# Gate columns summed on VectorE instead of multiplied on TensorE, and mixer steps given out by an account of VectorE's pending work

## The chip, the cores and the metric

The kernel runs on one core of a Trainium2 chip. The metric is device time in microseconds (us) of one execution. A core has engines that each work through their own queue of instructions in order: TensorE (PE in the profile, its weight loads PEld), VectorE (DVE), ScalarE (ACT), GpSimd (POOL) and SyncE (SP, which here only issues DMAs). They wait for each other by semaphores.

## The reference

One step of a diffusion backbone with one layer, 128 context tokens and 256 latent tokens, so T = 384 columns of tokens, with D = 4096 features.

```python
mod = (silu(c) @ w_ada + b_ada)            # for two conditions: c_ctx and c
shift, scale, gate = split(mod, 3)         # 4096 columns each
u = rms_norm(h, norm_w) * (1 + scale) + shift
proj = u @ w_in                            # 4096 x 16448
#   8 retention heads (q, k, v, g: 256 wide) and 16 gated DeltaNet heads (q, k, v, z: 128 wide)
#   DeltaNet: 5-tap conv on q, k, v; l2norm; chunked delta rule with a triangular solve;
#   both scans run forward and backward, from a cached state for the latent tokens
out = concat([o_ret, o_gdn]) @ w_out       # 4096 x 4096
h = h + gate * out
y = rms_norm(h, final_norm_w)
```

The outputs are y for both groups of tokens and the four new states of the context tokens. Only the third part of `mod`, the gate (4096 columns for two conditions), is touched by the arithmetic of the change. It is used at the very end, where the output projection is scaled by it.

## The kernel before

All large products are made in float32 with a split: each piece of weights (256 rows of one `raw` tile serve two pieces) is rounded on ScalarE (`wh`, `split_tile`, L210), the rest `wl = raw - wh` is made on VectorE (L211), and TensorE adds three products (L259 to L261 or L265 to L267) per tile of results. A piece is one step of 128 of the 4096 rows for 512 columns of weights. Four `raw` tiles, and five `wh` and five `wl` tiles, are in a ring, so weights are prepared some four pieces ahead of TensorE.

`run_pieces` walks through one long list of pieces, calls `prepare` of the pieces ahead and `compute` of the one in turn, and so sets the order of all queues when the program is built. The list has three stages:

1. Shift and scale of `mod` (class `Ada`, L323), and the first parts of the input projection as far as `u` is ready.
2. The remaining input projection: 32 groups of 512 columns, four for each p = 0 to 7. The first two give k, q and then v, z of the DeltaNet heads 2p and 2p+1 (kind "T", results 128x384), the other two q, k and v, gate of the retention head p (kind "N", results 128x512). When a group with k and q is done, the mixer that needs it (`gdn(p)` or `ret(p)`) is put on `bg_list`.
3. The output projection, eight groups of 512 columns. The mixers' outputs go through DRAM (`d_mix`) and come back in `mix_load`.

A mixer is a Python generator. Each `yield` ends a step: a few instructions on VectorE, ScalarE, TensorE (tiles named `bg`), GpSimd or a DMA. `gdn` has 127 steps: convolutions of k and q on VectorE (L645), norms, exponentials and masks, a triangular solve of 30 rounds on VectorE (L854 and L856, its input and output go through DRAM as `d_m` and `d_x`), merges of 32x32 blocks on TensorE, convolution of v, and the chunk products. `ret` has 34. A step leans on the one before it nearly everywhere.

Steps come into the queues in two ways. After every triple of products `slot(ns)` moves a planned clock on by 480 or 639 ns, and when the pause after the last step is over it calls `bg_step`, which takes one step of `urgent` or of the first mixer on `bg_list`. `pace` sets the pause from the step's declared cost, `PACE`, and the time left to the mixer's due time. The other way is `bg_drain(tag)`: it takes steps with nothing between them until that mixer is finished. It is called where something must be free or finished: in `new_raw` (eight result tiles, the oldest mixer's are wanted back), in `mix_load`, in `open_out`, and before a group of the output projection. Where the mixer is done already it does nothing.

Gate columns are made in stage 2 by eight `Ada` objects of 512 columns, 16 pieces each, mixed among the pieces of the groups of kind "N". A piece loads 512 KB of `w_ada` into a `raw` tile and issues four small products on four column strips of TensorE (tile `adg`, L323). At the end the four strips are copied (`gsb`, L1177), added by another product with `sel` (L1183), the bias is added (L1190) and the sums go to `d_gate` in DRAM.

Of the kernel before, what the change touches and what calls it, by code (L numbers as in the profile page):

```python
# [7 lines left out]
F32 = mybir.dt.float32  # L8
F32R = mybir.dt.float32r
AF = mybir.ActivationFunctionType  # L10
ALU = mybir.AluOpType
# [4 lines left out]
D = 4096  # L16
NK = 32
T = 384
# [26 lines left out]
PRE = 5  # L45
RING = 5
RAW_RING = 4
PACE = 1.4
CG = 166e3
CR = 45e3  # L50
COST = {"gates": 35e3, "gdn": CG, "ret": CR}
# [12 lines left out]

# [2 lines left out]
def hybrid_step(ctx: ExitStack, tc: tile.TileContext, x_prompt, x_sample, state_ret_fwd, state_ret_bwd,  # L67
# [33 lines left out]

    ident = const.tile([128, 128], F32, name="ident")
    half_c = const.tile([128, 2, 12], F32, name="half_c")
    mid_ctx = ExitStack()
# [5 lines left out]
    cst = mid.tile([128, 2 * NK + 32], F32, name="cst")  # L110
    sel = mid.tile([128, 2], F32, name="sel")
# [8 lines left out]
    rq_dec = mid.tile([128, 2, 2, 8], F32, name="rq_dec")  # L120
    rk_dec = mid.tile([128, 2, 8], F32, name="rk_dec")

    G.memset(half_c[:, 0], -0.5)
    G.memset(half_c[:, 1], 0.5)

# [20 lines left out]

    urgent = []

    clock = {"next": 0.0, "now": 0.0}
    left, due = {}, {}  # L150

    def pace(tag, ns):
# [13 lines left out]
    def bg_step():  # L166


        while urgent:
            try:  # L170
                return pace(("urgent", 0), next(urgent[0]))
# [14 lines left out]
    def slot(ns):  # L186
        clock["now"] += ns
        clock["next"] -= ns
        if clock["next"] <= 0:
            clock["next"] = max(clock["next"], -SLOT) + bg_step()  # L190


    def load_piece(src, chunks, k0, nk, ring=None):
        shape = [128, nk, len(chunks), chunks[0][1]]
# [6 lines left out]
                         in_=src[k0 * 128:(k0 + nk) * 128, c0:c0 + cn].rearrange("(k p) n -> p k n", p=128))  # L201
        return raw

    def split_tile(raw, shape, place=None):
# [5 lines left out]
        A.copy(h, raw)  # L210
        V.tensor_tensor(lo, raw, h.bitcast(F32), op=ALU.subtract)  # L211
        return h, lo

    class Gemm:
# [87 lines left out]
    class Ada:  # L302
# [3 lines left out]

        slots = 450.0

        def __init__(self, c0, width, ps_alloc, done, ring=None):
# [7 lines left out]
        def compute(self, i, raw):  # L317
            if self.ps is None:
                self.ps = self.ps_alloc()
            cs = slice(256 * (i // NK), 256 * (i // NK) + 256)  # L320
            for q in range(4):
                k = i % NK + q
                PE.matmul(self.ps[32 * q:32 * q + 32, cs], cst[:, 2 * k:2 * k + 32], raw[:, q, 0],  # L323
                          start=(k < 4), stop=(k >= NK - 4), tile_position=(0, 32 * q))
            slot(450)
            if i + 4 == self.width // 256 * NK:
                self.done(self.ps)
            return 1

    class Do:  # L330

# [16 lines left out]
    def run_pieces(pieces):  # L348

        t = 0.0  # L350
        for obj, i in pieces:
            if (id(obj), i) in dues:
                due[dues[id(obj), i]] = t
            t += obj.slots
        ready, nxt = {}, 0
        out = {"do": 0, "ada": 0, "w": 0}
        room = {"do": len(pieces), "ada": ADA_RING - 1, "w": RING - 1}
        kind = lambda o: "do" if isinstance(o, Do) else ("ada" if isinstance(o, Ada) and o.ring else "w")
# [21 lines left out]
    V.tensor_copy(sel, con[:, C_SEL:C_SEL + 2])  # L380

    def psb():
        return ps_st.tile([128, 512], F32, tag="s", name="s")
# [156 lines left out]
    def sum_done(g, partial, last):  # L540
# [9 lines left out]
        def done(n, ps):  # L550
            box = kept[g]
            if kind == "T":
                t = box[n // 2][:, T * (n % 2):T * (n % 2) + T]
                if partial:
                    V.tensor_tensor(t, ps, t, op=ALU.add)  # L555
                else:
                    A.copy(t, ps)
            else:
                for i in range(2):
                    t = box[i][:, 256 * n:256 * n + 256]  # L560
                    if partial:
                        V.tensor_tensor(t, ps[:, 256 * i:256 * i + 256], t, op=ALU.add)
                    else:
                        (A.copy if i else V.tensor_copy)(t, ps[:, 256 * i:256 * i + 256])  # L564
# [605 lines left out]
        yield  # L1170


    def gate_done(i):
        def done(ps):
            sb = [mx.tile([128, T], F32, tag="gsb", name="gsb", bufs=2)[:, 0:256] for _ in range(2)]
            for j in range(2):
                A.copy(sb[j], ps[:, 256 * j:256 * j + 256])  # L1177
            urgent.append(fin(ps, sb))

        def fin(ps, sb):  # L1180
            yield GATE
            for j in range(2):
                PE.matmul(ps[0:2, 256 * j:256 * j + 256], sel, sb[j], start=True, stop=True)  # L1183
            yield
            c0 = 512 * i
            for j in range(2):
                G.dma_start(out=sb[j][0:2], in_=b_ada[0, 2 * D + c0 + 256 * j:2 * D + c0 + 256 * j + 256].partition_broadcast(2))
            yield 2000
            for j in range(2):
                V.tensor_tensor(sb[j][0:2], ps[0:2, 256 * j:256 * j + 256], sb[j][0:2], op=ALU.add)  # L1190
                G.dma_start(out=d_gate[:, c0 + 256 * j:c0 + 256 * j + 256], in_=sb[j][0:2])
        return done
# [20 lines left out]
    ada_q = []  # L1213
    for i in range(8):
        ada_q += Ada(2 * D + 512 * i, 512, lambda: ps_main.tile([128, 512], F32, tag="mm3", name="adg"), gate_done(i)).pieces
    for g, (kind, chunks) in enumerate(groups):
        k0 = reached.get(g, 0)
        pre, done = sum_done(g, ("dram" if g >= 4 else "sbuf") if k0 else None, True)
        gm = Gemm(kind, w_in, chunks, list(range(k0, NK)), done, pre)
        if g % 4 == 0 and g:  # L1220
            dues[id(gm), max(0, len(gm.pieces) - PRE)] = ("gdn", g // 4 - 1)
        if kind == "T":
            pieces += gm.pieces
        else:
            n, rest = len(gm.pieces), 0
            if g % 2:
                rest = min(8, n // 2)
                cnt = len(ada_q) - 16 * (7 - g // 4)
            else:
                cnt = min(16, max(0, 16 * n // (n + NK - reached.get(g + 1, 0) - 8)))  # L1230
            pieces += gm.pieces[:LEAD] + interleave(gm.pieces[LEAD:n - rest], ada_q[:cnt]) + gm.pieces[n - rest:]
            ada_q = ada_q[cnt:]
    assert not ada_q
    rowk = [(2 * (j // 4) if j % 4 >= 2 else 16 + 2 * (j // 4)) + j % 2 for j in range(NK)]

    mixl = {}
# [14 lines left out]
    oc = {}  # L1251

    def open_out():
        bg_drain()
# [25 lines left out]
    def out_done(c0):  # L1280
# [3 lines left out]
        def pre():  # L1284
            if not oc:
                open_out()
            bg_drain(("out", c0 - 512))
            op = oc["sb"]
            box["x"] = op.tile([128, 3, 512], F32, tag="xo", name="xo", bufs=1)
            box["g"] = op.tile([128, 2, 512], F32, tag="go", name="go")  # L1290
            box["w"] = op.tile([128, 512], F32, tag="wo", name="wo")
# [22 lines left out]
    def place(i):  # L1314
# [2 lines left out]
        return m >= 0 and [t[m].rearrange("p k t -> p (k t)")[:, 0:512].rearrange("p (a b) -> p a b", a=2)  # L1317
                           for t in (uh, ul)]

    for i in range(8):  # L1320
        pre, done = out_done(512 * i)
        gm = Gemm("N", w_out, [(512 * i, 256), (512 * i + 256, 256)], list(range(NK)), done, pre,
# [5 lines left out]
        if i == 0:  # L1328
# [4 lines left out]
            for j, piece in enumerate(seq):  # L1333
                for m, fn in ((j - 2, mix_put), (j, mix_load)):
                    if 0 <= m < NK:
                        pieces += Do(lambda m=m, fn=fn: fn(m)).pieces
                pieces.append(piece)
        else:
            pieces += gm.pieces
    run_pieces(pieces)  # L1340
    bg_drain()

# [50 lines left out]
```

## Time and profile before

| | |
|---|---|
| median of 3 runs | 3338.46 us (3335.72 to 3339.66) |
| profiled execution, its own time | 3342.99 us |
| its span, first to last instruction | 3340.9 us |
| TensorE busy | 97% of the span |
| VectorE busy | 55% |
| ScalarE busy | 36% |
| GpSimd busy | 9% |
| granted clock of TensorE, mean | 0.994 |

Busy time is the time in which an engine has at least one instruction under way. A row of a group gives count, busy time and mean duration, and behind the second bar the engine's idle time just before those instructions with what ended most of it. Durations on one engine can overlap a little, so count times mean can exceed the busy time.

### The profile page before, as it was taken

How to read it: one execution, taken by the hardware profiler on the slowest of the kernel's cores; microseconds unless marked ns; L12 is line 12 of the kernel's file. 1: busy time of each engine (PE TensorE's matmuls, PEld its weight loads, DVE VectorE, ACT ScalarE, POOL GpSimd, SP SyncE). 2: the span in 40 equal slices, each digit the busy share in tenths (PEclk: the TensorE clock that was granted, in tenths of full speed). 3: DMA queues.
4: the chain of work that ended last, by engine and by line, in shares of the span. 5: the costliest groups of instructions: out<-in, count | busy, mean ns of one | idle time of the engine just before them, and what ended most of it. 6: DMA issues, size and time to landing. Idle time of an engine off the chain costs nothing. (4 is left out here: it accounts for less than half of the span.)

```text
span 3340.9 us, 51824 instructions
## 1 busy us (share of the span) xinstructions
PE 3256.4 (97%) x19312; PEld 2706.2 (81%) x19312; DVE 1840.7 (55%) x3811; ACT 1198.9 (36%) x2588; POOL 292.2 (9%) x463
## 2 busy tenths in 40 slices
PE   5999999999999999999999999999999999999998
PEld 2778888877699779789789779779779877788887
DVE  2554433335855756754856746746844845444444
ACT  3322222224245235244345245235244334333333
POOL 0000000001101001001011001011000012100000
PEclk9999999999999999999999999999999999999999
DMA  9888998975534554544645645554644556645444
GB/s 304 290 287 272 330 311 266 297 251 159 179 105 135 169 153 149 179 145 140 192 146 152 185 129 156 173 154 147 177 153 141 160 153 188 187 145 170 145 151 170
DMA packets 594236, 626.14 MB, mean 187 GB/s; under 512 B 38978, under 2 KB 577042, under 8 KB 593984
## 3 DMA queue, kind: packets, MB, share of 16 engines
q1 hardware_dynamic: 570096, 551.04, 52.7%
q0 software_dynamic: 23888, 71.79, 7.3%
q8 instruction: 151, 2.47, 0.3%
q14 instruction: 101, 0.83, 0.1%
HBM read 590.37 MB, written 32.33 MB: 186 GB/s over the span
## 5 line engine op out<-in xcount | busy, mean ns | idle before, releaser
L211 DVE TENSOR_TENSOR wl<-raw,wh 128x512 fp32r<-128x512 f32 x1274 | 854.3, 687 | 939.8 <-ACT wh L210 935.8
L210 ACT CAST wh<-raw 128x512 fp32r<-128x512 f32 x1274 | 756.6, 620 | 1350.6 <-DMA raw<-in_w_in_dram 659.0
L265 PE MATMUL mm<-wh,uh 128*128 128x512 f32 x1920 | 784.3, 408 | 9.1 <-ACT rawt L564 5.6
L266 PE MATMUL mm<-wl,uh 128*128 128x512 f32 x1920 | 755.3, 393 | 6.4 <-DVE wl L211 5.8
L267 PE MATMUL mm<-wh,ul 128*128 128x512 f32 x1920 | 752.9, 392 | 0.0
L259 PE MATMUL mm<-uh,wh 128*128 128x384 f32 x2048 | 721.0, 352 | 6.2 <-DVE ul L555 3.8
L261 PE MATMUL mm<-uh,wl 128*128 128x384 f32 x2048 | 689.4, 337 | 0.0
L260 PE MATMUL mm<-ul,wh 128*128 128x384 f32 x2048 | 688.8, 336 | 0.0
L265 PEld LDWEIGHTS mm<-wh,uh 128*128 128x128 f32 x1920 | 362.2, 189 | 141.0 <-issue 48.2
L259 PEld LDWEIGHTS mm<-uh,wh 128*128 128x128 f32 x2048 | 387.3, 189 | 51.2 <-issue 34.6
L266 PEld LDWEIGHTS mm<-wl,uh 128*128 128x128 f32 x1920 | 362.7, 189 | 81.2 <-DVE wl L211 14.1
L267 PEld LDWEIGHTS mm<-wh,ul 128*128 128x128 f32 x1920 | 362.2, 189 | 78.2 <-DVE ul L1248 0.7
L260 PEld LDWEIGHTS mm<-ul,wh 128*128 128x128 f32 x2048 | 387.6, 189 | 3.9 <-issue 2.9
L261 PEld LDWEIGHTS mm<-uh,wl 128*128 128x128 f32 x2048 | 386.8, 189 | 0.0
L854 DVE TENSOR_TENSOR tmp<-M 48x4 f32<-48x4 f32 (+14 forms) x240 | 189.3, 789 | 3.4
L323 PE MATMUL ada<-adar,cst 128*32 128x256 f32 x2048 | 147.5, 404 | 26.9 <-DMA adar<-in_w_ada_dram 26.9
L645 DVE SCALAR_TENSOR_TENSOR acc<-rawt,cw,acc 128x126 f32<-128x126 f32 (+3 forms) x384 | 133.8, 413 | 12.8 <-ACT acc L640 12.8
L266 PE MATMUL o<-wl,uh 128*128 128x512 f32 x354 | 138.1, 390 | 0.2 <-DVE wl L211 0.2
L265 PE MATMUL o<-wh,uh 128*128 128x512 f32 x354 | 138.0, 390 | 0.2 <-ACT wh L210 0.2
L267 PE MATMUL o<-wh,ul 128*128 128x512 f32 x354 | 137.9, 390 | 0.0
L323 PEld LDWEIGHTS ada<-adar,cst 128*32 128x32 f32 x2048 | 53.8, 112 | 92.7 <-DMA adar<-in_w_ada_dram 42.8
L856 DVE TENSOR_REDUCE M<-tmp 48x2 f32<-48x4 f32 (+14 forms) x240 | 121.6, 507 | 8.3
(321 smaller groups left out, 2522.7 us busy)
## 6 DMA issues: line engine op xcount, KB each, us to landing
raw<-in_w_in_dram SPq DMA_DIRECT2D x1028, 256.0 KB, 3.6
adar<-in_w_ada_dram SPq DMA_DIRECT2D x256, 512.0 KB, 5.7
raw<-in_w_ada_dram SPq DMA_DIRECT2D x128, 512.0 KB, 4.3
raw<-in_w_out_dram SPq DMA_DIRECT2D x256, 256.0 KB, 3.1
rawt<-d_part POOLq DMA_DIRECT2D x26, 384.0 KB, 4.3
d_part<-spill POOLq DMA_DIRECT2D x9, 768.0 KB, 7.4
gr<-d_gc POOLq DMA_DIRECT2D x16, 384.0 KB, 7.4
d_mix<-rawt POOLq DMA_DIRECT2D x32, 192.0 KB, 2.8
```

The source lines that it names most:

```text
L210: A.copy(h, raw)
L211: V.tensor_tensor(lo, raw, h.bitcast(F32), op=ALU.subtract)
L259: PE.matmul(ps, wh, high(k), start=st, stop=False)
L260: PE.matmul(ps, wh, low(k), start=False, stop=False)
L261: PE.matmul(ps, wl, high(k), start=False, stop=sp)
L265: PE.matmul(ps, a, h, start=st, stop=False)
L266: PE.matmul(ps, a, lo, start=False, stop=False)
L267: PE.matmul(ps, b, h, start=False, stop=sp)
L323: PE.matmul(self.ps[32 * q:32 * q + 32, cs], cst[:, 2 * k:2 * k + 32], raw[:, q, 0], start=(k < 4), stop=(k >= NK - 4), tile_position=(0, ...
L645: V.scalar_tensor_tensor(out=dst[:, lo:hi], in0=x[:, lo + o:hi + o], scalar=w(t), in1=dst[:, lo:hi], op0=ALU.mult, op1=ALU.add)
L854: V.tensor_tensor(t, M[0:48, 0:i, 0:i].rearrange("p j c -> p c j"), M[0:48, i:i + 1, 0:i].to_broadcast([48, i, i]), op=ALU.mult)
L856: V.tensor_reduce(M[0:48, i, 0:i], t, axis=AX.X, op=ALU.add)
```

## The change

The gate columns leave TensorE. A new class `GateSum` loads two row blocks of 384 columns of `w_ada` (384 KB, 16 loads per object) and adds each block, times the condition's value of that row, to a running sum on VectorE: two conditions, so four instructions of 128x384 per load, and for 4096 columns eleven objects with 704 instructions in all (64 of them 256 columns wide). At an object's end four small products with a tile of ones add over the partitions, and the bias and the store to `d_gate` follow. Half of a load's sums are put off behind the next split (`later`). Seven objects are mixed among the four groups of p = 1 to 7, four among groups 1 to 6 of the output projection.

The steps of mixers are given out by another rule. `clock["dve"]` is an account of when VectorE will be done with what was issued: each split, each sum and each step adds a declared cost. `slot` now takes a step only where that account is less than `BACKLOG` = 1500 ns ahead of the planned clock. `bg_drain` has no such condition, and its steps are put on the account too. The pause is also set otherwise: `PACE` 1.4 to 1.0, `FMAX` 1.0 to 2.0, and smaller declared totals.

```diff
-PACE = 1.4
-CG = 166e3
-CR = 45e3
+PACE = 1.0
+CG = 130e3
+CR = 28e3
+SPLIT = 690.0
+STEP = 300.0
+BACKLOG = 1500.0
-FMAX = 1.0
+FMAX = 2.0
+GATE_W = 384
+GATE_END = 10
...
+    def dve(ns):
+        clock["dve"] = max(clock["dve"], clock["now"]) + ns
...
         while bg_list:
             tag, job = bg_list[0]
             try:
-                return pace(tag, next(job))
+                ns = next(job)
+                dve(STEP if ns is None or ns < 0 else ns)
+                return pace(tag, ns)
...
     def slot(ns):
         clock["now"] += ns
         clock["next"] -= ns
-        if clock["next"] <= 0:
+        if clock["next"] <= 0 and clock["dve"] - clock["now"] < BACKLOG:
             clock["next"] = max(clock["next"], -SLOT) + bg_step()
...
         V.tensor_tensor(lo, raw, h.bitcast(F32), op=ALU.subtract)
+        dve(SPLIT)
+        if later:
+            later.pop(0)()
...
+    class GateSum:
+        def prepare(self, i):
+            raw = load_piece(w_ada, [(2 * D + self.c0, self.width)], i, 2)
...
+            def add(q):
+                for v, acc in enumerate(self.acc):
+                    dve(1.5 * self.width)
+                    a, w = acc[:, 0:self.width], cst[:, 2 * (i + q) + v:2 * (i + q) + v + 1]
+                    if i + q == 0:
+                        V.tensor_scalar(a, raw[:, q, 0], scalar1=w, scalar2=None, op0=ALU.mult)
+                    else:
+                        V.scalar_tensor_tensor(out=a, in0=raw[:, q, 0], scalar=w, in1=a, op0=ALU.mult, op1=ALU.add)
...
+        def fin(self):
...
+            ps = ps_main.tile([128, T // 2], F32, tag="mm3", name="gsum")
+            for r, v, o in parts:
+                PE.matmul(ps[r:r + 32, 0:n], ones, self.acc[v][:, o:o + n], start=True, stop=True, tile_position=(0, r))
...
-    def gate_done(i):
...
+    gate_sums = [GateSum(c0, min(GATE_W, D - c0)).pieces for c0 in range(0, D, GATE_W)]
...
+        if p:
+            gp = gp[:LEAD] + interleave(gp[LEAD:-GATE_END], gate_sums.pop(0)) + gp[-GATE_END:]
...
+            pieces += interleave(behind, [p for ps in gate_sums for p in ps]) + gm.pieces
```

The order of the queues changes at many places. The first shown is TensorE's queue in `gdn(5)`, between the merges of blocks. Before, the mixer's products (`bg`) stand one step at a time between products of the projection (`mm`); L916 and L926 are two merges.

```order
L265 MATMUL mm_20195<-wh,uh_1784 128x512
L266 MATMUL mm_20195<-wl,uh_1784 128x512
L267 MATMUL mm_20195<-wh,ul_1785 128x512
L926 MATMUL bg<-U,P_20388 64x64 x12
L265 MATMUL mm_20196<-wh,uh_1784 128x512
L266 MATMUL mm_20196<-wl,uh_1784 128x512
L267 MATMUL mm_20196<-wh,ul_1785 128x512
```

In the changed kernel the same merge (now L1005) stands among the mixer's other products, from the first transposes (L858) to the last; there is no `mm` row in this stretch of 164 products.

```order
L972 MATMUL bg<-P_20727,U 32x32 x6
L977 MATMUL bg<-U,P_20727 32x32 x12
L995 MATMUL bg<-x_0_7127,U 64x64 x6
L995 MATMUL bg<-x_1_7128,U 64x64 x6
L1005 MATMUL bg<-U,P_20786 64x64 x12
L1029 MATMUL bg<-ident,rawt 128x128 x6
L1046 MATMUL bg<-S,rawt 128x128 x4
L1062 MATMUL bg<-rawt,U 128x128 x2
```

So the mixer's products moved from between the pieces into one place. The second place is VectorE's queue in the same mixer, in the last rounds of the solve. Before, splits (`wl`) for coming pieces stand between the rounds.

```order
L854 TENSOR_TENSOR tmp<-M 48x841
L856 TENSOR_REDUCE M<-tmp 48x29
L211 TENSOR_TENSOR wl<-raw,wh 128x512
L854 TENSOR_TENSOR tmp<-M 48x900
L856 TENSOR_REDUCE M<-tmp 48x30
L211 TENSOR_TENSOR wl<-raw,wh 128x512 x2
```

In the changed kernel the rounds follow each other, and the transposes of the solve's result and the copies of merges (L966, L984, L999) follow them, with no split in between.

```order
L933 TENSOR_TENSOR tmp<-M 48x841
L935 TENSOR_REDUCE M<-tmp 48x29
L933 TENSOR_TENSOR tmp<-M 48x900
L935 TENSOR_REDUCE M<-tmp 48x30
L933 TENSOR_TENSOR tmp<-M 48x961
L935 TENSOR_REDUCE M<-tmp 48x31
L947 STREAM_TRANSPOSE U<-x_0_7127 32x6x32
```

The splits moved out of the solve to the stretch ahead of it. The third place is that stretch on VectorE, ahead of `gdn(5)`: sums (`gacc`) and splits stand there, seventeen splits in a row, then copies of a group's results (L643).

```order
L378 SCALAR_TENSOR_TENSOR gacc<-raw,cst,gacc 128x384 x2
L230 TENSOR_TENSOR wl<-raw,wh 128x512 x4
L378 SCALAR_TENSOR_TENSOR gacc<-raw,cst,gacc 128x384 x4
L230 TENSOR_TENSOR wl<-raw,wh 128x512 x17
L643 COPY rawt<-mm_19882 128x256
```

No step of a mixer is in these rows: the steps that stood between splits moved behind them, into `gdn(5)`'s one stretch.

Over the whole program, `bg_drain` finds unfinished mixers at fourteen places in stage 2 and at the start of stage 3, where before it found none: the last 51, 46, 57, 98, 119, 125, 125 and 125 of the 127 steps of `gdn(0)` to `gdn(7)`, and the last 33 of the 34 steps of `ret(2)` to `ret(7)` each stand in one piece.

More of the change, by code (lines that the diff above doesn't have):

```diff
@@ L47 @@
 RAW_RING = 4
-PACE = 1.4
-CG = 166e3
-CR = 45e3
-COST = {"gates": 35e3, "gdn": CG, "ret": CR}
+PACE = 1.0
[4 more added lines that the diff above has]
+BACKLOG = 1500.0
+COST = {"gates": 26e3, "gdn": CG, "ret": CR}
 FMIN = 0.5
@@ L103, in hybrid_step @@
     half_c = const.tile([128, 2, 12], F32, name="half_c")
+    ones = const.tile([128, 32], F32, name="ones")
+    cst = const.tile([128, 2 * NK + 32], F32, name="cst")
     mid_ctx = ExitStack()
@@ L147, in hybrid_step @@
     urgent = []
-    clock = {"next": 0.0, "now": 0.0}
+    clock = {"next": 0.0, "now": 0.0, "dve": 0.0}
+    def dve(ns):
+        clock["dve"] = max(clock["dve"], clock["now"]) + ns
     left, due = {}, {}
@@ L328, in compute, with __init__ @@
             return 1
+    class GateSum:
+        slots = 0.0
+        def __init__(self, c0, width):
+            self.c0, self.width = c0, width
+            self.pieces = [(self, i) for i in range(0, NK, 2)]
+        def prepare(self, i):
+            raw = load_piece(w_ada, [(2 * D + self.c0, self.width)], i, 2)
+            if i == 0:
+                while urgent and not oc:
+                    bg_step()
+                tag = (lambda v: f"ga{v}") if oc else (lambda v: "gsb")
+                self.acc = [(oc["sb"] if oc else mx).tile([128, T], F32, tag=tag(v), name="gacc", bufs=2)
+                            for v in range(2)]
+            def add(q):
[6 more added lines that the diff above has]
+                        V.scalar_tensor_tensor(out=a, in0=raw[:, q, 0], scalar=w, in1=a, op0=ALU.mult, op1=ALU.add)
+            while later:
+                later.pop(0)()
+            add(0)
+            if i + 2 < NK:
+                later.append(lambda: add(1))
+            else:
+                add(1)
+        def compute(self, i, hl):
+            if i + 2 == NK:
+                urgent.append(self.fin())
+            return 1
+        def fin(self):
+            n, sb = self.width // 2, self.acc[0]
+            parts = [(32 * q, q // 2, n * (q % 2)) for q in range(4)]
+            yield GATE
+            ps = ps_main.tile([128, T // 2], F32, tag="mm3", name="gsum")
+            for r, v, o in parts:
+                PE.matmul(ps[r:r + 32, 0:n], ones, self.acc[v][:, o:o + n], start=True, stop=True, tile_position=(0, r))
+            yield
+            for r, v, o in parts:
+                c0 = 2 * D + self.c0 + o
+                G.dma_start(out=sb[r:r + 32, 0:n], in_=b_ada[0, c0:c0 + n].partition_broadcast(32))
+            yield 2000
+            V.tensor_tensor(sb[:, 0:n], ps[:, 0:n], sb[:, 0:n], op=ALU.add)
+            for r, v, o in parts:
+                G.dma_start(out=d_gate[v:v + 1, self.c0 + o:self.c0 + o + n], in_=sb[r:r + 1, 0:n])
+            clock["gate"] = self.c0 + self.width
     class Do:
@@ L357, in run_pieces @@
         room = {"do": len(pieces), "ada": ADA_RING - 1, "w": RING - 1}
-        kind = lambda o: "do" if isinstance(o, Do) else ("ada" if isinstance(o, Ada) and o.ring else "w")
+        kind = lambda o: "do" if isinstance(o, (Do, GateSum)) else ("ada" if isinstance(o, Ada) else "w")
         for idx, (obj, i) in enumerate(pieces):
@@ L1170, in ret @@
         yield
-    def gate_done(i):
[L1174 to L1192, printed above, removed]
     def gates_done(ps):
@@ L1212, in hybrid_step @@
     pieces += Do(open_mixers).pieces + Gates(gates_done).pieces
[L1213 to L1233, printed above, removed]
+    gate_sums = [GateSum(c0, min(GATE_W, D - c0)).pieces for c0 in range(0, D, GATE_W)]
+    for p in range(8):
+        gp = []
+        for g in range(4 * p, 4 * p + 4):
+            kind, chunks = groups[g]
+            k0 = reached.get(g, 0)
+            pre, done = sum_done(g, ("dram" if g >= 4 else "sbuf") if k0 else None, True)
+            gm = Gemm(kind, w_in, chunks, list(range(k0, NK)), done, pre)
+            if g % 4 == 0 and g:
+                dues[id(gm), max(0, len(gm.pieces) - PRE)] = ("gdn", g // 4 - 1)
+            gp += gm.pieces
+        if p:
+            gp = gp[:LEAD] + interleave(gp[LEAD:-GATE_END], gate_sums.pop(0)) + gp[-GATE_END:]
+        pieces += gp
     rowk = [(2 * (j // 4) if j % 4 >= 2 else 16 + 2 * (j // 4)) + j % 2 for j in range(NK)]
@@ L1288, in pre @@
             op = oc["sb"]
+            assert clock["gate"] >= c0 + 512
             box["x"] = op.tile([128, 3, 512], F32, tag="xo", name="xo", bufs=1)
```

18 lines of the change are left out of this document (11 added, 7 removed).

## The prediction

> **What bounds the kernel now.** I read the page's busy shares and costliest groups first, then the windows by stage, because the change touches stage 2 (about 790 to 2790 us) and stage 3.
>
> ```profile
> span 3340.9 us, 51824 instructions
> ...
> PE 3256.4 (97%) x19312; PEld 2706.2 (81%) x19312; DVE 1840.7 (55%) x3811; ACT 1198.9 (36%) x2588; POOL 292.2 (9%) x463
> ...
> L211 DVE TENSOR_TENSOR wl<-raw,wh 128x512 fp32r<-128x512 f32 x1274 | 854.3, 687 | 939.8 <-ACT wh L210 935.8
> ```
>
> TensorE is busy throughout. VectorE's largest group, the splits, waits 936 us for ScalarE, which in turn waits for free tiles: the preparation of weights runs ahead and is paced by TensorE. The windows (busy us and count for PE, PEld, DVE, ACT, POOL, then granted clock, DMA share, GB/s) say the same by stage.
>
> ```profile
> core 0: us, PE busy (x) PEld busy (x) DVE busy (x) ACT busy (x) POOL busy (x), PEclk, DMA share, GB/s
> 0.00:100.00 100.00, 58.11 (x396) 33.26 (x397) 31.59 (x83) 31.34 (x99) 4.66 (x14) 0.93 0.97 310
> 790.00:2790.00 2000.00, 1982.23 (x11730) 1666.68 (x11729) 1250.08 (x2700) 788.82 (x1799) 230.57 (x346) 1.00 0.52 157
> 2880.00:3320.00 440.00, 440.00 (x1942) 364.40 (x1941) 188.94 (x284) 146.96 (x262) 20.64 (x36) 1.00 0.49 152
> ```
>
> In stage 2 TensorE stands still for only 18 us of 2000, although 16 mixers with hundreds of hand-overs run there. They cost nothing but their own products because, in the queue, each step stands between pieces of the projection. This is the cover that the change has to leave in place. So the sum is: what leaves TensorE, plus what now stops it.
>
> **What leaves TensorE.** A gate piece in TensorE's timeline (start, duration):
>
> ```profile
> 2635.66 0.39 PE L266 MATMUL mm<-wl,uh 128*128 128x512 f32 x1
> 2635.89 0.39 PE L267 MATMUL mm<-wh,ul 128*128 128x512 f32 x1
> 2636.20 0.64 PE L323 MATMUL adg<-raw,cst 128*32 128x256 f32 x8
> 2636.77 0.50 PE L265 MATMUL mm<-wh,uh 128*128 128x512 f32 x1
> 2637.11 0.40 PE L266 MATMUL mm<-wl,uh 128*128 128x512 f32 x1
> 2637.35 0.39 PE L267 MATMUL mm<-wh,ul 128*128 128x512 f32 x1
> ...
> L323 PE MATMUL adg<-raw,cst 128*32 128x256 f32 x1024 | 81.8, 391 | 0.0
> ```
>
> From one L267 to the next is 1.46 us; three usual starts 0.23 apart make 0.68, so the piece costs 0.78, times 128 pieces 100 us. Its busy time alone is 82. I take 90, since a few pieces stand beside a mixer's product and share its gap. The eight `sel` groups go and eleven groups of four products with `ones` come: equal, within a few us. Also gone at no gain: 16 copies on ScalarE.
>
> **What is added on VectorE.** The nearest row for a sum is the same operation on 384 columns, and there is the smaller form in the convolution:
>
> ```profile
> L1053 DVE SCALAR_TENSOR_TENSOR rawt<-bg,gnw,rawt 128x384 f32<-128x384 f32 x16 | 9.8, 614 | 6.2 <-PE bg L1051 5.8
> L645 DVE SCALAR_TENSOR_TENSOR acc<-rawt,cw,acc 128x126 f32<-128x126 f32 (+3 forms) x384 | 133.8, 413 | 12.8 <-ACT acc L640 12.8
> ```
>
> 704 by 0.614 is 432 us, of it 275 in stage 2 (448 sums) and 157 in stage 3. VectorE then has 1525 of some 1910 us in stage 2 and 346 of 440 in stage 3, about 80% in both. With four pieces (8 us of TensorE) prepared ahead and half of a load's sums put off behind a split, I cost them at nothing. If that cover failed, the bound is 1.2 us per load, 176 loads, 211 us. SP's queue has 176 loads of 384 KB in place of 128 of 512 KB, at a DMA share near 0.5; a `raw` tile is given back after two sums instead of after TensorE's turn, so I see no loss there.
>
> **What the new rule does to the mixers.** A piece advances the planned clock by 1.92 us. The account gets 0.69 for its split, and per p 64 sums of 0.58, 37 us. With 770 splits in stage 2 (row below), some 96 pieces per p, 0.85 us a piece or 82 us per p is left under the limit. The declared steps of a pair of mixers are more: 34 us for the solve (30 times 390 ns and 2.1 ns times the squares), 16 for convolutions, about 40 for the other steps of `gdn`, 13 for `ret`, together about 103. So steps fall behind, the next `new_raw` drains the rest at once, and that cost goes on the account while the planned clock stands still. The account is then tens of us ahead, `slot` gives nothing out for that long, and the next mixer is later still. The order shows the result: 14 stretches, growing from half a `gdn` to nearly all of it.
>
> In a stretch TensorE's queue holds the mixer's products and nothing else, and behind them the pieces that could run. Every hand-over of the mixer is then time in which TensorE stands. The splits of the next four pieces are already ahead of the stretch on VectorE, and the last of them waits for a tile that TensorE frees about 1 us before it comes to the stretch; so VectorE starts on the mixer only then.
>
> **The price of one stretch.** I add up what is not TensorE's in the chain of one whole `gdn`; TensorE's own products were paid before too.
>
> ```profile
> 790.00:2790.00 2000.00, 1572.03 (x5217) 960.33 (x5217) 517.51 (x770) 456.05 (x769) 1.00 0.52 157
> 790.00:2790.00 2000.00, 301.49 (x2848) 253.35 (x2848) 172.24 (x520) 156.08 (x579) 1.00 0.52 157
> L854 DVE TENSOR_TENSOR tmp<-M 48x4 f32<-48x4 f32 (+14 forms) x240 | 189.3, 789 | 3.4
> L856 DVE TENSOR_REDUCE M<-tmp 48x2 f32<-48x4 f32 (+14 forms) x240 | 121.6, 507 | 8.3
> L555 DVE TENSOR_TENSOR rawt<-mm,rawt 128x384 f32<-128x384 f32 x120 | 63.9, 553 | 43.5 <-PE mm L261 43.3
> L562 DVE TENSOR_TENSOR rawt<-mm,rawt 128x256 f32<-128x256 f32 x54 | 20.0, 418 | 11.5 <-PE mm L267 11.4
> L564 DVE COPY rawt<-mm 128x256 f32<-128x256 f32 x45 | 18.4, 419 | 33.3 <-PE mm L267 33.3
> L822 ACT ACTIVATE gr<-gr,gt_ngc 128x128 f32<-128x128 f32 x96 | 29.8, 389 | 0.1
> L989 ACT ACTIVATE wk<-bg,br 128x128 f32<-128x128 f32 x96 | 26.5, 377 | 65.8 <-PE bg L983 65.8
> L135 POOL TENSOR_TENSOR rs<-ss,half_c 128x12 f32<-128x12 f32 x8 | 20.0, 2497 | 248.1 <-DVE ss L789 248.1
> L862 POOL DMA_DIRECT2D x<-d_x x32 | 18.5, 577 | 24.1 <-DMA d_x<-M 24.1
> d_m<-dd POOLq DMA_DIRECT2D x32, 48.0 KB, 2.6
> M<-d_m POOLq DMA_DIRECT2D x8, 192.0 KB, 3.3
> d_x<-M POOLq DMA_DIRECT2D x8, 192.0 KB, 3.0
> x<-d_x POOLq DMA_DIRECT2D x32, 24.0 KB, 5.1
> ```
>
> The first row is the instructions on `wh` tiles (PE, PEld, the splits on DVE, the rounding on ACT), the second those on `bg` tiles, in the same order.
>
> - VectorE. 1250 less 518 for splits and 102 for taking over results (L555, L562, L564) is 630, or, with a little off for biases and one-off work, 78 per pair; 12 of it are `ret`'s (30 instructions near 0.4), so 66 for `gdn`. In this busy time neighbours overlap (L645: 384 times 413 ns would be 159, not 134). In a chain they can't: the solve's rows (189.3 and 121.6, 38.9 per mixer) are exactly count times mean. By counts and means all of `gdn` is 87. Between 66 and 87 I take 81, near the chain.
> - DMA. The trip to `d_m` and back: three issues, 2.6 and 3.3. To `d_x` and back: 3.0, seven issues of 0.58, 5.1. With hand-overs to GpSimd 21 us.
> - GpSimd. The powers, 2.5 and 1.3 (half the elements): 4.
> - ScalarE. 789 less 456 and some 30 for results is 303, 38 per pair, 28 of it `gdn`'s by busy time and 34 by counts and means (exponentials L822, scalings L989, squares, copies). What VectorE can't run beside I count, step by step, at 22; bounds 0 and 34.
> - TensorE's products are 301/8 or 38 per pair, 25 for `gdn`; of these 16 stand in the chain and 9 beside other work, which I take off.
> - Slow clock. In the first 100 us, where TensorE is busy 58% and the granted clock 0.93, the same product lasts up to 637 ns instead of 379:
>
> ```profile
> L323 PE MATMUL ada<-adar,cst x2048: 378/379/637, 10.2 to 728.7; 128*32 128x256 f32 x187
> ```
>
> That is 1.68 times. In a stretch TensorE is mostly idle, so 16 us of products become 27, and the first pieces behind it lose about 2: plus 13. The Trainium skill, "TensorE: Matmul & The Clock Gate", Part 1, The HAM clock gate, states that after an idle window of about 3.4 us the array gets half of the clock pulses until it was busy as long. By that rule the term would be 16 and 2, some 5 us more in a full stretch, 35 in all, and the time 4145. The row's ratio, below 2, fits it in part.
>
> Together 81+21+4+22-9+13 = 132, less 2 steps done and 1 us of overlap at the front about 128. By parts: up to the masks 21, masks, exponentials and first trip 24, solve with its gaps 41, second trip, merges, convolution of v and outputs 44.
>
> So the `gdn` stretches cost: 125 steps three times, 3 x 128 = 384; 119 steps 124; 98 steps (first part done) 106; 57 steps (the last six rounds, 16, and the last part) 60; 51 steps (trip mostly over) 36; 46 steps 32. Sum 742. A `ret` stretch: VectorE 12, ScalarE 5, GpSimd 1.3, slow clock 8, less 6 for products in the shade and the front: 20, six times 120. In all 862.
>
> In stage 3 the results' steps (9 instructions of 0.69 on VectorE per group) also stand in one place, five pieces ahead of the next group's end; 6 us there lie under the four prepared pieces: nothing, at worst 2 us per group.
>
> **Sum.** 3340.9 - 90 + 862 = 4113 in span. The profiled execution took 3342.99 by its own time, 4.5 above the median of 3338.46, and 2 lie outside the span: 4110 for the median.
>
> **Rivals.**
> 1. Short stops. The engines run a mixer side by side: ScalarE hidden, VectorE at 66, no slow clock. A full stretch is 66+21+4-9-3 = 79, the stretches 0.62 times as long, 530, and the time 3780. Against it: a step reads what the step before wrote. A half-way case ends at 3945.
> 2. Long stops. Nothing overlaps: 87+21+4+34+18-3 = 161, 1.26 times, 1085, time 4335.
> 3. Faster. TensorE finds the stretches' work ready, so only the gate's products count. For that the 14 stops must average less than 90/14 = 6.4 us, a sixth of the shortest one I work out; the time would be 3250. For it speaks only that drained steps were covered in stage 2 before; but then none were drained.
> 4. The account does what it says and VectorE at 80% is what delays splits: 3250 plus up to 211, so 3250 to 3460. The order, with whole mixers in one place, speaks against it.
>
> **How the numbers follow.** Forecast near 4110 with VectorE and ScalarE as chosen: 0.70. Rival 1, whole or half, 0.14; rival 2, 0.12; rival 3, 0.02; rival 4, 0.02. The range leaves out the far ends of 1 and 2 and takes in half of each: 3920 to 4300. Less than 0.2% could not be told from no change; slower is 0.97, same 0.01, faster 0.02.
>
> **What would show it.** Right: in the profile after, TensorE idle near 30% in stage 2, its busy share of the span near 77%, the idle time put down to VectorE, ScalarE and DMA before `bg` products; eight long gaps of growing length, the solve of 39 us as a bare stretch of VectorE; slices with granted clock below 0.9; no `adg`; sums at 0.55 to 0.61 us with splits still ahead of TensorE outside the gaps. Wrong: gaps under 30 us at late mixers, or `wl` as what TensorE waits for between stretches.

## The result, and the profile after

The changed kernel takes 3931.51 us (median of four runs, 3929.62 to 3934.17); the kernel before took 3339.06 us beside it. The ratio is 1.1772 (95% interval 1.1752 to 1.1792), so 592 us slower. The forecast was 4110 us, 771 us slower; direction and mechanism came as forecast, the size was 179 us too large, and the time lies only 11 us above the lower end of the stated range (3920 to 4300). The profiled execution took 3934.17 us.

The page of the changed kernel: the span, the busy time of each engine, then TensorE's busy tenths and its granted clock in 40 slices of 98 us.

```profile
span 3932.3 us, 51061 instructions
...
PE 3278.8 (83%) x18344; PEld 2789.2 (71%) x18344; DVE 2219.2 (56%) x4509; ACT 1222.0 (31%) x2572; POOL 318.7 (8%) x520
...
PE   5999999998998996982996499189929991799998
...
PEclk9999999999998997995998699589959995899999
...
L230 DVE TENSOR_TENSOR wl<-raw,wh 128x512 fp32r<-128x512 f32 x1274 | 856.8, 688 | 951.3 <-ACT wh L229 938.7
...
L288 PE MATMUL mm<-wl,uh 128*128 128x512 f32 x1920 | 754.0, 393 | 3.4 <-DVE wl L230 3.3
...
L378 DVE SCALAR_TENSOR_TENSOR gacc<-raw,cst,gacc 128x384 f32<-128x384 f32 (+1 forms) x682 | 379.6, 599 | 19.3 <-DMA raw<-in_w_ada_dram 19.1
...
L959 PE MATMUL bg<-x,U 32*32 32x32 f32 x384 | 20.8, 226 | 333.1 <-DMA x<-d_x 325.1
```

TensorE, busy nearly throughout before, has slices at 1, 2 or 4 tenths from the middle of the run on, and in the same slices its clock falls to 0.5 or 0.6. The splits (L230) still run ahead, and TensorE's products with `wl` (L288) wait 3.4 us in all. The largest part of the new loss is in one row: the first products behind the solve (L959) have 333 us of idle time ahead of them. In the kernel before, the same products (there L880) had none:

```profile
L880 PE MATMUL bg<-x,U 32*32 32x32 f32 x384 | 13.4, 193 | 0.0
```

VectorE, with 378 us more busy time, is busy 56% of the span against 55% before, since the span grew too.

TensorE's waits give the same in another form (total us, times, longest). A wait is put down to the last thing that ended it, so the first row, "DMA", holds the trips through DRAM, the whole solve on VectorE between them, and the trip back.

```profile
PE bg L959 <- DMA x<-d_x: 325.1, 12, 62.0
PE bg L1029 <- ACT rawt L1021: 54.1, 16, 6.3
PE bg L1130 <- ACT o L1125: 36.9, 8, 4.8
PE bg L1174 <- DVE rawt L1165: 31.0, 12, 7.4
```

The windows show stage 2 and then one stretch, that of `gdn(5)`, in its parts: the whole, the front up to the norms, masks and exponentials, the trip through `d_m`, the solve, the trip through `d_x`, and merges to outputs.

```profile
core 0: us, PE busy (x) PEld busy (x) DVE busy (x) ACT busy (x) POOL busy (x), PEclk, DMA share, GB/s
790.00:3410.00 2620.00, 2059.31 (x11022) 1802.80 (x11021) 1550.68 (x3236) 849.19 (x1857) 258.28 (x401) 0.86 0.39 116
...
2458.35:2588.60 130.25, 37.35 (x306) 32.32 (x305) 79.53 (x195) 31.88 (x102) 15.26 (x21) 0.57 0.06 16
2458.35:2481.20 22.85, 6.64 (x25) 4.85 (x24) 13.55 (x44) 7.56 (x31) 2.82 (x2) 0.61 0.12 41
2481.20:2491.30 10.10, 3.30 (x12) 2.71 (x12) 8.31 (x30) 8.23 (x25) 0.77 (x1) 0.50 0.00 0
2491.30:2500.00 8.70, 0.00 (x0) 0.00 (x0) 1.47 (x6) 0.03 (x1) 3.06 (x5) 0.50 0.23 45
2500.00:2539.70 39.70, 0.00 (x0) 0.00 (x0) 37.35 (x61) 0.00 (x0) 0.00 (x0) 0.50 0.00 0
2539.70:2550.40 10.70, 2.11 (x36) 1.87 (x36) 2.94 (x8) 0.00 (x0) 5.05 (x9) 0.50 0.16 37
2550.40:2588.60 38.20, 25.31 (x233) 22.89 (x233) 15.91 (x52) 16.07 (x47) 3.55 (x5) 0.68 0.02 8
```

TensorE stands for 561 of 2620 us of stage 2 (18 of 2000 before). In the row of the solve VectorE works alone for 39.7 us; in the two trips little is busy.

### The profile page after: what moved, and what is told of

Read it like the earlier page. It is cut to its first block, busy times and chain, and to the rows that moved or that the text cites. A ratio compares the mean times of both kernels' runs of the same rounds, so it can differ in the third digit from the quotient of the medians.

```text
span 3932.3 us, 51061 instructions
## 1 busy us (share of the span) xinstructions
PE 3278.8 (83%) x18344; PEld 2789.2 (71%) x18344; DVE 2219.2 (56%) x4509; ACT 1222.0 (31%) x2572; POOL 318.7 (8%) x520
## 5 line engine op out<-in xcount | busy, mean ns | idle before, releaser
L230 DVE TENSOR_TENSOR wl<-raw,wh 128x512 fp32r<-128x512 f32 x1274 | 856.8, 688 | 951.3 <-ACT wh L229 938.7
L229 ACT CAST wh<-raw 128x512 fp32r<-128x512 f32 x1274 | 766.8, 621 | 1632.8 <-PE mm L289 568.6
L287 PE MATMUL mm<-wh,uh 128*128 128x512 f32 x1920 | 762.0, 397 | 20.1 <-ACT wh L229 11.7
L288 PE MATMUL mm<-wl,uh 128*128 128x512 f32 x1920 | 754.0, 393 | 3.4 <-DVE wl L230 3.3
L281 PE MATMUL mm<-uh,wh 128*128 128x384 f32 x2048 | 710.4, 347 | 14.2 <-DVE ul L633 3.8
L288 PEld LDWEIGHTS mm<-wl,uh 128*128 128x128 f32 x1920 | 363.9, 190 | 80.8 <-DVE wl L230 7.1
L378 DVE SCALAR_TENSOR_TENSOR gacc<-raw,cst,gacc 128x384 f32<-128x384 f32 (+1 forms) x682 | 379.6, 599 | 19.3 <-DMA raw<-in_w_ada_dram 19.1
L959 PE MATMUL bg<-x,U 32*32 32x32 f32 x384 | 20.8, 226 | 333.1 <-DMA x<-d_x 325.1
L959 PEld LDWEIGHTS bg<-x,U 32*32 32x32 f32 x384 | 18.2, 139 | 336.8 <-issue 299.5
L933 DVE TENSOR_TENSOR tmp<-M 48x4 f32<-48x4 f32 (+14 forms) x240 | 180.8, 754 | 6.4
L288 PE MATMUL o<-wl,uh 128*128 128x512 f32 x354 | 139.0, 393 | 1.7 <-DVE wl L230 1.7
```

Of the source, the lines that this page charges most:

```text
L281: PE.matmul(ps, wh, high(k), start=st, stop=False)
L287: PE.matmul(ps, a, h, start=st, stop=False)
L288: PE.matmul(ps, a, lo, start=False, stop=False)
L378: V.scalar_tensor_tensor(out=a, in0=raw[:, q, 0], scalar=w, in1=a, op0=ALU.mult, op1=ALU.add)
L933: V.tensor_tensor(t, M[0:48, 0:i, 0:i].rearrange("p j c -> p c j"), M[0:48, i:i + 1, 0:i].to_broadcast([48, i, i]), op=ALU.mult)
```

## The experiments

The theories are named by letters in the expectations. **A**: the loss is the stretches of mixer steps with nothing between them; the sums themselves cost little. **B**: the loss is VectorE's added work, which delays splits. **A2** and **A3** came up after the first four runs: in a kernel without stretches the sums do cost something, by A2 because they come to VectorE where it is already full (in the solves), by A3 about the same per sum wherever they stand. The runs of the kernel before that stand beside each group of experiments had medians from 3335.28 to 3336.94 us; ratios are to those.

**One stretch by itself (held_gdn5).** The kernel before, with `gdn(5)` held after two steps until a drain takes the other 124; gate on TensorE, nothing else changed.

```diff
...
-        if clock["next"] <= 0:
+        if clock["next"] <= 0 and not (not urgent and bg_list and bg_list[0][0] == HELD and taken[0] >= 2):
...
```

> The kernel before, with one change: after its first two steps gdn(5) gets no step until it is drained, so 124 of its 127 steps stand in one place, with no sums anywhere. Theory A as measured in the changed kernel: a gap of 118 to 125 us on TensorE, less the 21 us that its products cost in between before: 3336 plus 97 to 104, 3433 to 3440. Theory A as forecast (128 net): 3464. Theory B (stretches are not what costs): 3336.

Measured: 3439.73 us, ratio 1.0311 (1.0295 to 1.0328), 103 us slower. Its windows have the stretch as one row, beside a quiet stretch of projection:

```profile
2230.70:2353.40 122.70, 36.44 (x305) 31.55 (x305) 74.85 (x185) 31.58 (x102) 15.26 (x21) 0.57 0.05 13
2000.00:2200.00 200.00, 200.00 (x1049) 167.80 (x1048) 75.64 (x127) 61.39 (x108) 8.22 (x14) 1.00 0.56 175
```

With no sum and no account in the program, one drained `gdn` makes nearly the same hole as in the changed kernel (130.2 us there). It is 122.7 us long; some 21 us of it were paid before as TensorE's own products. That the stretch is the loss is shown, and the forecast's 128 for a full one is too high by 25.

**The gate's products left out (gate_left_out).** The kernel before, without the gate's loads and products; the bias alone goes to `d_gate`.

```diff
...
-    for i in range(8):
+    for i in range(0):
...
```

> The kernel before without the gate's products (the gate is the bias alone, so the output is not the reference's): the price of the gate on TensorE by itself. By the delays between projection products in the traces, 77 us: 3255 to 3262. As forecast, 90 (82 to 100): 3236 to 3254.

Measured: 3255.23 us, ratio 0.9761 (0.9746 to 0.9776), 82 us faster. The removed work is worth 82, not 90.

**The sums without the new rule (sums_only).** The changed kernel with the old way of giving out steps.

```diff
-PACE = 1.0
-CG = 130e3
-CR = 28e3
+PACE = 1.4
+CG = 166e3
+CR = 45e3
...
-FMAX = 2.0
+FMAX = 1.0
...
-        if clock["next"] <= 0 and clock["dve"] - clock["now"] < BACKLOG:
+        if clock["next"] <= 0:
```

> Gate columns as sums on VectorE, with the old rule for the steps (pauses and totals of before, no limit by the account). No step is drained in this order. Theory A (the loss comes from the mixers that stand in one place): 3339 less the 82 to 100 us of the gate pieces, 3240 to 3260. Theory B (the 700 sums on VectorE delay the splits): most of the loss stays, above 3600.

Measured: 3381.08 us, ratio 1.0142 (1.0127 to 1.0158), 46 us slower. Neither theory had this. 82 us went with the gate's products, so the sums cost about 128 us here. The group rows and windows say where. The rows are the products with `wl` before and here; the windows are the solve of one `gdn` here, then, in a view of the sums' tile alone that has no column for ACT, the sums in it, and last the same solve in the kernel before.

```profile
L266 PE MATMUL mm<-wl,uh 128*128 128x512 f32 x1920 | 755.3, 393 | 6.4 <-DVE wl L211 5.8
...
L288 PE MATMUL mm<-wl,uh 128*128 128x512 f32 x1920 | 767.0, 399 | 68.2 <-DVE wl L230 67.7
```

```profile
2645.50:2706.40 60.90, 52.34 (x211) 37.94 (x210) 59.52 (x99) 14.78 (x24) 0.00 (x0) 1.00 0.40 121
...
2645.50:2706.40 60.90, 0.00 (x0) 0.00 (x0) 9.09 (x16) 0.00 (x0) 1.00 0.40 121
```

```profile
2623.70:2675.00 51.30, 51.30 (x259) 38.45 (x259) 49.91 (x81) 12.79 (x21) 0.00 (x0) 1.00 0.57 175
```

Before, the solve already kept VectorE busy 49.9 of 51.3 us (97%) with TensorE busy throughout. Sixteen sums add 9.1 us; the solve takes 9.6 us longer, and TensorE stands for 8.6 us, waiting for `wl`. Over the eight solves TensorE is idle 68 of 477 us, against 7 of 418 before.

**Only the limit taken out (no_account).** The changed kernel, with its new numbers, without the account's condition in `slot`.

```diff
-        if clock["next"] <= 0 and clock["dve"] - clock["now"] < BACKLOG:
+        if clock["next"] <= 0:
```

> The changed kernel with its new pauses and totals, but without the condition on the account in slot. Only the last 22 steps of ret(7) are drained. Theory A: 3250 plus some 10 us for that stretch, 3255 to 3275. Theory B: above 3600.

Measured: 3395.35 us, ratio 1.0181 (1.0166 to 1.0196). One condition is worth 536 of the 592 us. The new numbers cost 14 over sums_only, and with them comes the one drained stretch of `ret(7)`, a hole of 20.6 us of which some 10 were paid before; the miss against the expectation is again the sums.

**The new rule without the sums (rule_only).** The kernel before, gate on TensorE, with the account, the limit and the new numbers.

```diff
...
-        if clock["next"] <= 0:
+        if clock["next"] <= 0 and clock["dve"] - clock["now"] < BACKLOG:
```

> The kernel before with the gate columns on TensorE, with the new pauses, totals, account and limit. Without the sums on the account the order has three short stretches: 22 steps of gdn(0), 2 of gdn(3), 24 of ret(7). Theory A: about 33 us of stretches, of which 12 are products that were paid before, so 3339 plus 20, 3350 to 3370: the rule alone does little harm, it needs the sums on its account. Theory B: 3339, since no sum is there.

Measured: 3364.66 us, ratio 1.0095 (1.0077 to 1.0113), 29 us slower. Only 22 steps of `gdn(0)`, two of `gdn(3)` and 24 of `ret(7)` are drained. Without the charge for the sums the rule leaves enough room for the steps.

**Drained steps not charged (drain_free).** The changed kernel, where `bg_drain` puts the account back to what it was.

```diff
     def bg_drain(tag=None):
+        was = clock["dve"]
...
+        clock["dve"] = was
```

> The changed kernel, but steps that bg_drain takes are not left on the account. The order then has gdn stretches of 51, 20, 35, 58, 46, 51, 28 and 5 steps and one of 29 steps of ret, in place of 51 to 125 and six of ret. Theory A, with the gaps measured in the changed kernel for such lengths (38, 14, 26, 60, 37, 38, 20, 3, 20, together 256, less about 110 of products paid before): 3250 plus 146, 3370 to 3430. So two thirds of the loss would come from charging drained steps to a clock that stands still. Theory B: above 3600.

Measured: 3438.73 us, ratio 1.0307 (1.0290 to 1.0324), 9 above the expected band. The stretches stay, but at 51, 20, 35, 58, 46, 51, 28 and 5 steps of the `gdn` and 29 of one `ret`, and do not grow. So the self-feeding of the rule (a drain is charged, so that the next mixer starts later and is drained longer) is worth 493 us, the limit as such 43 (3395 to 3439). These 43 are a balance. The stretches here leave holes of some 268 us between projection products, of which the expectation counts about 110 as paid before; in return TensorE hardly waits for splits. Its waits for `wl` (total us, times, longest), first in no_account, then here:

```profile
PE mm L288 <- DVE wl L230: 63.0, 64, 3.6
...
PE mm L290 <- DVE wl L232: 3.5, 8, 0.9
```

So here the limit did keep the splits on time, and the holes were its price. That is why the expectation, which put the sums at nothing, was only 9 us off.

**An account that gives the steps room (fair_account).** As drain_free, and a quarter of each time step is also taken off the account, with `FMAX` 1.0. No mixer is drained.

```diff
...
+        clock["dve"] -= 0.25 * ns
...
```

> The changed kernel with three edits to the rule: drained steps are not left on the account, the account runs down by a quarter more than the planned clock (which leaves out the mixers' products), and FMAX is 1.0. No step is drained in this order, and the sums stay on VectorE in stage 2. Theory A2 (sums cost where they meet the solve's long steps, and a limit that holds steps back avoids that): TensorE's delays fall by half, 3310 to 3345. Theory A3 (the solve's steps are too long for any such limit, a sum is paid wherever it stands): as sums_only, 3370 to 3395.

Measured: 3396.61 us, ratio 1.0178 (1.0159 to 1.0197). This is 52 us above A2's band and 2 above A3's: the half of A2 by which a limit that holds steps back avoids the cost did not come true. The limit now costs nothing against no_account, and brings nothing: TensorE is idle 74 of 481 us in the solves, against 76 of 472 there. Why a limit of 1500 ns does not keep the splits on time there was not found.

**Each sum twice (sums_twice).** sums_only with each sum after the first of a column made a second time into a tile that nobody reads.

```diff
...
+                        V.scalar_tensor_tensor(out=self.junk[:, 0:self.width], in0=raw[:, q, 0], scalar=w, in1=a, op0=ALU.mult, op1=ALU.add)
```

> sums_only with each sum after the first of a column done twice, the second time into a tile that nobody reads. Stage 2 then has 1250 + 2 x 275 = 1800 us for VectorE in some 1960, the solves far over. Theory A2: about twice the excess in the solves and new excess elsewhere, 3381 plus 150 to 300, 3530 to 3680. Theory A3 (0.16 per sum): 3381 plus 110, 3490.

Measured: 3634.99 us, ratio 1.0895 (1.0873 to 1.0916), 254 us over sums_only. The first 704 sums cost about 128, the next 682 twice that, though VectorE is busy only 1371.6 of 1750 us in the middle:

```profile
1000.00:2750.00 1750.00, 1569.06 (x8445) 1344.01 (x8444) 1371.59 (x2800) 623.90 (x1394) 194.58 (x299) 0.96 0.44 133
...
L288 PE MATMUL mm<-wl,uh 128*128 128x512 f32 x1920 | 785.7, 409 | 136.3 <-DVE wl L230 134.9
```

The cost rises faster than the count, which the even price of A3 (3490) does not give. TensorE's idle time in the solves goes from 68 to 125 us, about twice, as A2 has it. But much of the new cost lies elsewhere: stage 3, from its first product to the end, takes 559 us against 493 in sums_only. So the solves are the first place where VectorE runs out of room, and not the only one.

**Solve steps further apart (solve_wide).** sums_only with the declared cost of a solve step times 1.6 and `PACE` 1.2.

```diff
...
-            yield 390.0 + 2.1 * i * i
+            yield 1.6 * (390.0 + 2.1 * i * i)
```

> sums_only with the solve's steps declared 1.6 times as long and PACE 1.2 in place of 1.4, so that a solve is spread over half as much time again; nothing is drained in this order. Theory A2 (in the solve VectorE is full already, and the sums there are what delays splits): the 68 us that TensorE stands idle in the eight solves fall to 10 to 25, 3325 to 3345. Theory A3 (a sum costs its 0.16 us anywhere in stage 2): 3370 to 3385 as sums_only.

Measured: 3350.99 us, ratio 1.0040 (1.0027 to 1.0054), 30 us under sums_only and 6 above the expected band. TensorE's idle time in the solves falls from 68 to 38 us, and its wait for splits from 67.7 to 17.1:

```profile
L288 PE MATMUL mm<-wl,uh 128*128 128x512 f32 x1920 | 758.7, 395 | 17.4 <-DVE wl L230 17.1
```

Where the same sums and steps stand looser, 30 us come back. That is the direct evidence for the place. The solves came out 16% longer (553 us in all against 478), not half as long again, and VectorE is as full in them as before (67.8 of 69.1 us in the last one); what fell is the number of solve steps per piece. Of the 128 us, 61 are idle time in the solves. Some 20 lie in stage 3, which takes 493 us from its first product to the end in sums_only, against 471 in the kernel before and 472 in gate_left_out. The rest does not show as idle time: from start to start, the projection's products lose some 76 us in the solves against gate_left_out, and some 35 spread over the rest of stage 2. What delays these 35 was not found.

**Sums only where VectorE has room (sums_late).** The kernel before with the old rule; five `Ada` objects (2560 columns) stay on TensorE in stage 2, and four `GateSum` objects (1536 columns) stand in stage 3.

```diff
-    for i in range(8):
+    for i in range(5):
...
+            pieces += interleave(behind, [p for ps in gate_sums for p in ps]) + gm.pieces
```

> Old rule; five eighths of the gate columns on TensorE as before, the last 1536 columns as four sums objects in stage 3 alone, where no mixer runs. Theory A2: saves 77 x 3/8 = 29 us and costs the 12 us of delay that stage 3 shows in the kernel with all sums and the old rule, 3315 to 3325. Theory A3 (the same price for a sum wherever it stands, 112 us over 704 sums): 29 saved, 41 paid, 3345 to 3350.

Measured: 3319.33 us (six runs), ratio 0.9948 (0.9934 to 0.9962). This is the best version, 17 us faster than the kernel before, and inside A2's band (A3 had it slower than the kernel before).

```profile
2880.00:3290.00 410.00, 405.85 (x1798) 330.76 (x1796) 284.82 (x486) 129.49 (x238) 33.12 (x62) 1.00 0.66 205
```

In stage 3 VectorE is busy 69% with the sums, and TensorE stands for 4 us of 410. Three eighths of 82 are 31 us, and 17 came, so the sums there cost some 14. From its first product to the end the stage takes 487 us against 471 before, which is 16.

**Both (late_wide).** sums_late with the solve steps set as in solve_wide. 

> sums_late with the same wider solve. Theory A2: in stage 2 no sum stands, and before the solves cost only 7 us of idle time there, so 0 to 7 us less than sums_late, 3312 to 3320. If the wider solve by itself is worth more than that, A2 has the wrong reason for solve_wide.

Measured: 3328.47 us (12 runs), ratio 0.9980 (0.9972 to 0.9989). It is 9 us slower than sums_late and 8 above the expected band. Without sums beside the solve the wider setting is no gain, so the gain of solve_wide is not the setting's own; what the 9 us are was not found.

**The changed kernel without most of its sums (no_sums).** Order, loads and charges to the account stay; of each condition's 32 sums per column only the first is made.

```diff
                     if i + q == 0:
                         V.tensor_scalar(a, raw[:, q, 0], scalar1=w, scalar2=None, op0=ALU.mult)
-                    else:
-                        V.scalar_tensor_tensor(out=a, in0=raw[:, q, 0], scalar=w, in1=a, op0=ALU.mult, op1=ALU.add)
```

> The changed kernel with the same order, account and loads, but of each column's 32 sums only the first is done (the gate is wrong, so the output is not the reference's); the declared costs stay. Theory A (in the changed kernel the mixers stand in stretches, so between them VectorE has room and the sums are free but for a few at the front of a stretch and in stage 3): 3931 less 15 to 50 us, 3880 to 3916. Theory B' (the sums cost here what they cost with the old rule, 110 to 120 us): 3810 to 3820.

Measured: 3918.64 us, ratio 1.1746 (1.1723 to 1.1770), 13 us under the changed kernel.

```profile
PE 3273.1 (84%) x18344; PEld 2789.8 (71%) x18344; DVE 1878.2 (48%) x3827; ACT 1225.2 (31%) x2572; POOL 319.0 (8%) x520
...
L957 PE MATMUL bg<-x,U 32*32 32x32 f32 x384 | 20.9, 226 | 330.6 <-DMA x<-d_x 322.4
```

341 us less on VectorE, and the wait before the merges is the same. In the changed kernel the sums' time costs 13 us (9 by the two ratios, and their intervals overlap); it is their charge on the account that costs hundreds.

## Why the prediction was right, and where its sizes were off

**The mechanism held, the size was near the edge.** The measured 3931 is closer to the half-way case of rival 1 (3945, which with the whole of rival 1 had a chance of 0.14) than to 4110; that it lies inside the range owes something to luck. The forecast read from the order that whole mixers would stand in one place of TensorE's queue and that TensorE would then stand for the length of their chain. held_gdn5 shows this for one stretch, rule_only and drain_free that the stretches come from the sums' charges and from charging drains, and no_sums that the sums' own time has little part in it. The changed kernel has 14 holes longer than 20 us between projection products, the eight of `gdn` (37.7, 36.8, 60.1, 107.5, 118.7, 130.2, 124.6, 130.4 us) and six of `ret` (21.7 to 26.2), 887 us together.

**The term of the `gdn` stretches was mis-sized: 742 forecast, some 584 measured.** The eight holes are 746 us; TensorE's own products in them, about 21 us for a full one and 19 for the three short ones by the delays they caused before, were paid already. The hole of a full stretch, 152 us by the forecast's terms (81+21+4+22 and 27 of slowed products, less 3), took 130, and 3 of that are sums and splits at its front. Counting each moment once, in the order VectorE, ScalarE, TensorE, GpSimd, the hole of `gdn(5)` is made of 79.5 us of VectorE (76.3 without those 3, where 81 was forecast), 18.0 of ScalarE while VectorE is idle (22), 13.1 of TensorE while both are idle (27), 6.8 of GpSimd by itself and 12.8 with nothing busy (25 for these two). Over half of the excess is the term of TensorE. The choice that failed was "16 stand in the chain": TensorE is busy 37.4 us in the hole, slowed from about 25, but most of it lies beside VectorE or ScalarE, where slowness costs nothing. VectorE at 81 was chosen near the chain's value of 87; 76.3 (74.9 in held_gdn5, which has no sums) is about midway to the lower bound of 66. The forecast had ruled out that neighbours on VectorE overlap in a chain, but in the convolutions they do: these sixteen instructions in the hole took 5.33 us, and by their group's mean of 0.41 us they would take 6.6.

```profile
2467.58 5.33 DVE L724 SCALAR_TENSOR_TENSOR acc<-rawt,cw,acc 128x126 f32<-128x126 f32 x16 [1.16 <-ACT acc L719]
```

The three short stretches were forecast at 128 and cost about 78: they hold the last steps, where 268 of the mixer's 304 products stand, so most of what had been paid before lies in them.

**The `ret` stretches: 120 forecast, 83 measured** (141 us of holes, less some 58 paid before), in part for the same reason: in these holes TensorE is busy 15 to 16 us, but only about 6 of them while VectorE and ScalarE are idle, so the slow clock's 8 us each lay largely in the shade. VectorE is busy 10 to 11 us there, where 12 was forecast.

**The gate: 90 forecast, 82 measured** by gate_left_out. In the changed kernel the balance is 667 for the stretches, less these 82, plus the 13 of no_sums: 598, where 592 was measured. The parts are good to a few us each.

**"I cost them at nothing" was right only beside the stretches.** sums_only has the sums cost about 128 us, over half the bound of 211, by the delayed splits of rival 4. The step that failed looked at VectorE's mean of 80% in a stage; in the solves VectorE stood at 97% before, and there the cover of four prepared pieces did not suffice. Had the changed rule spread the steps as meant, rival 4 would have been the outcome (3381 in sums_only, 3397 in fair_account). In the changed kernel the steps stand in the holes, not between the splits, and the same sums cost 13.

**The slow clock** is there as forecast: granted 0.50 through the solve and 0.57 over the hole. Behind the hole the projection's products start like this (start, duration), against the group's mean:

```profile
2589.03 0.52 PE L282 MATMUL mm<-ul,wh 128*128 128x384 f32 x1
2589.35 0.52 PE L283 MATMUL mm<-uh,wl 128*128 128x384 f32 x1
...
L282 PE MATMUL mm<-ul,wh 128*128 128x384 f32 x2048 | 692.5, 338 | 0.0
```

0.52 against 0.338 us is 1.54 times. The granted 0.50 agrees with the half of the pulses that the Trainium skill, "TensorE: Matmul & The Clock Gate", Part 1, The HAM clock gate, states for an idle array; the time that the forecast worked out from it, 4145, was further off, since the slowed products were mostly hidden. How much the slow clock costs by itself was not tried.

**The signs.** As forecast: no `adg`; sums at 0.60 us on average; a bare solve of 39.7 us on VectorE; slices under 0.9 of the clock; growing holes; products with `wl` hardly waiting between them. Off with the size: TensorE idle 21% of stage 2 (30 forecast) and busy 83% of the span (77).

## What to carry to other kernels

The hand-overs of a serial chain cost TensorE nothing here only while every step stood between pieces of other work in its queue: a drain that takes the rest at once turns each hand-over into time in which the engine stands, so a limit that holds steps back must be read together with what drains them, and drained steps must not be charged against the next ones. Read an engine's room from the stage's tightest stretch (97% in the solve), not from its mean (62% in stage 2); the same sums cost about 128 us with the old rule, about half of it in the solves, some 14 to 16 for three eighths of them in stage 3 alone, and about 13 beside holes. In the price of a hole count only what no other engine covers: most of the slowed products here lay beside VectorE or ScalarE.

## What the runs showed of the hardware that had not been expected

The second set of sums cost twice the first (254 against about 128 us) while VectorE's busy share of the span rose only from 65% to 71%. The granted clock stays at 0.50 in the trip through `d_x` although 36 products stand there (2.1 us busy of 10.7), and the 0.68 of the last part of the hole is a mean of two levels:

```profile
2550.40:2572.80 22.40, 14.30 (x157) 13.36 (x158) 9.84 (x31) 6.66 (x14) 0.00 (x0) 0.50 0.01 1
2572.80:2586.40 13.60, 9.38 (x71) 8.46 (x70) 5.46 (x20) 7.33 (x28) 3.55 (x5) 1.00 0.06 20
```

TensorE was busy 64% of the first stretch under half the clock, and 69% of the second under the full one. Then the clock went back to 0.50, and it stayed there for the first 4.7 us behind the hole, though TensorE was busy without a break. So a share of busy time alone does not tell the clock, and a mean clock hides when it changed.
